# Chunk sums of the x1 squares on VectorE, norm rows and output tokens by other transposes, in a one-core streaming encoder layer

## The chip, the core and the metric

The kernel runs on one core of a Trainium2 chip. The metric is the device time in microseconds of one execution, taken as the median of several runs. The profile below is of one execution, recorded by the hardware profiler; its rows name instructions by the line of the kernel (L1307 is line 1307), by engine (PE is TensorE's matmul, PEld its weight load, DVE is VectorE, ACT is ScalarE, POOL is GpSimd, SP issues DMAs) and by the program's tile names.

## The reference, cut to what matters

One layer of an encoder works on 1024 prompt tokens and 32 sample tokens, 1056 in all, with 1024 features:

```
h = RMSNorm(x); z = h @ W_in                 # queries, keys, gates ...
A: windowed attention;  B: gated linear recurrence
m = sigmoid(gA) * (y_A @ W_brA) + sigmoid(gB) * (y_B @ W_brB)
x = x + RMSNorm(m @ W_out)                   # this x is "x1" in the kernel
[a | u] = RMSNorm(x) @ W_up;  a = causal depthwise conv3(a)
x = x + RMSNorm((gelu(a) * u) @ W_down)      # this x is "x2"
y = x + (p @ W_ple) * sigmoid(x @ W_ple_gate)
```

RMSNorm divides each token by the root of the mean of its squares over the 1024 features and scales each feature. All data are float32.

## The kernel before, in words

Inside the kernel the data lie transposed: features on the 128 partitions (1024 features are 8 chunks of 128) and tokens along the free dimension. Each product is split into high and low parts, so that each block of weights takes three matmuls (lines 202 to 204, 1735 to 1737, 2014 to 2016, 2105 to 2107). From the W_out product on, the 1056 tokens are four groups of 264 (`H`); groups 0 and 1 are a pair, and so are groups 2 and 3.

The instructions are not issued in the order of the text. A scheduler puts them in order on each engine, by their order in the text and by when its model thinks their inputs ready. `behind(engine)` (line 88) ties what it encloses, on that engine, behind the instruction of that engine that was traced last: it can't be issued earlier, but it waits for nothing else. `mm`, `tr` and `st` tiles are PSUM banks; there are two `tr` banks and three `st` pairs.

The parts that the change touches:

- **Norm rows** (`norm_rows`, line 298). A norm is a column: one value a token, tokens on partitions. The kernel needs it as rows, the same value on all 128 partitions. It takes the column, broadcast to 128 columns, as the weights of a matmul and the identity as the moving operand. It is called with three pieces for each group: at the start for the first RMSNorm (three groups of up to 3 x 128 tokens), by `pair_norm` (two groups of 3 x 88 tokens, so six calls; four pair norms in all) and by `x2_rows` (six calls, twice).
- **The x1 sums of the second pair.** `x1_half` (line 1329) adds the normed W_out product onto x; the result, x1 of groups 2 and 3, lies in `x1q[g]`, two halves of 4 chunks x 264 tokens, in a page of a large pool (`lq`) that an operand part of the up stage takes over later. `last_ops` (line 1698), called after each of the seven steps of the first half of up unit 0, squares it in place on ScalarE (line 1703, steps 2 and 4) and calls `x1_sums(2)` at step 5. `x1_sums` (line 1711) calls `sums88` (line 1302): for each of three pieces of 88 tokens, eight matmuls, one for each chunk, with the squares as weights and a single column of ones as the moving operand, accumulate the sum of squares into one PSUM column (line 1307). `x1_sums(3)` comes after the first step of the second half, then `pair_norm(1, ...)`: VectorE turns the sums into reciprocal roots (line 1318 and `rsqrt`, lines 213 to 219). The rows follow behind the fifth step. The first pair's squares are added over chunks on VectorE before the sums (`x1_squares`, line 1354).
- **Up unit 0** (`up_unit`, line 1717). 22 units make the up projection by seven products each (Strassen's scheme). Unit 0 is done in two halves, pair 0 then pair 1, each of seven steps of 12 matmuls, since pair 1's operands (`build_ops(1)`, lines 1379 and 1380) are still being made; `next(op1)` makes one part of them. After a step, `after` (line 1742) evacuates PSUM on VectorE (lines 1748, 1750, 1753, 1755, 1757, 1762, 1764). From the fifth step of the second half on, VectorE also prepares unit 1's weights.
- **The output stage** (line 2087). For each half h of the tokens and each chunk c of 128 features, 16 blocks in all, 48 matmuls with W_ple_gate, then tanh on ScalarE and two operations on VectorE give `y`, features on partitions, 2 x 264 tokens. One block later `y_done` (line 2054) turns it: six transposes of 88 tokens into two `tr` banks (line 2064), two ScalarE copies into `yr` tiles (line 2075), and, after each odd chunk, stores of two chunks' columns (lines 2077 to 2080) from SP's queue, which also loads the `ple` blocks (line 2043) and the x1 blocks (line 1949). The y tiles have the tag "t" with four buffers, shared with these x1 blocks. The very last block is turned piece by piece, so that its stores start early.

## Time and profile before

| | |
|---|---|
| median of three runs | 2006.07 us (2005.35 to 2007.28) |
| the profiled execution | 2008.97 us, of which its span 2006.5 us |
| mean granted TensorE clock over the span | 0.993 |
| up units (L1735) | 1192.2 to 1659 us |
| down product (L2014) | 1659.6 to 1893 us |
| output stage (L2105) | from 1893.5 us |
| mean DMA rate | 139 GB/s |

How to read it: the profile gives for each engine its busy time and the number of its instructions; "idle before, releaser" says how long the engine stood before an instruction and what it waited for. In a timeline row stand the start, the duration, engine, line, operation, written and read tiles, shapes and how many rows were merged. A matmul's duration includes its way through the array, which overlaps with the next one, so the cost of a matmul in the queue is the distance between starts, not the duration. A float32 product shows as two records of weight load and matmul where it isn't marked float32r, and a transpose as one.

### The profile page before, as it was taken

What the parts mean: (1) busy time and instruction counts of PE and PEld (TensorE: products, weight loads), DVE (VectorE), ACT (ScalarE), POOL (GpSimd) and SP (SyncE); (2) the same over time, 40 slices, a digit from 0 to 9 for tenths busy, and PEclk for the clock granted to TensorE, in tenths of its full rate; (3) what the DMA queues carried; (4) which work ended last, traced back from release to release, by engine and by line L of the source; (5) the groups of instructions that cost most, each with busy time, mean ns of one, the idle gap of its engine ahead of it and who ended that gap; (6) DMA issues with size and microseconds to landing.
All of it is one profiled execution on the core that took longest, in us unless ns stands there. A gap on an engine that the chain in (4) does not pass through costs nothing. (4 is left out here: it accounts for less than half of the span.)

```text
span 2006.5 us, 38869 instructions
## 1 busy us (share of the span) xinstructions
PE 1977.5 (99%) x14858; PEld 1946.1 (97%) x14858; DVE 1466.2 (73%) x3187; ACT 975.8 (49%) x2224; POOL 286.0 (14%) x386
## 2 busy tenths in 40 slices
PE   7999999999999999999999999999999998999998
PEld 6999999999999999999999999999999998999998
DVE  5788888688888888644455777787878886677852
ACT  5655556556666666542124653333333344534532
POOL 2010100000000000002100022545454431000000
PEclk9999999999999999999999998999999999999999
DMA  8322321321111111377656693564555669889543
GB/s 262 94 97 69 106 73 52 136 64 47 47 42 46 54 56 56 119 215 233 195 167 198 215 315 83 114 145 117 141 128 128 141 171 284 257 261 267 151 112 84
DMA packets 334498, 278.12 MB, mean 139 GB/s; under 512 B 15512, under 2 KB 317867, under 8 KB 333672
## 3 DMA queue, kind: packets, MB, share of 16 engines
q1 hardware_dynamic: 312114, 234.94, 39.3%
q0 software_dynamic: 22128, 40.65, 9.0%
q8 instruction: 116, 1.90, 0.4%
q14 instruction: 70, 0.57, 0.1%
q10 hardware_dynamic: 70, 0.06, 0.0%
HBM read 186.48 MB, written 89.11 MB: 137 GB/s over the span
## 5 line engine op out<-in xcount | busy, mean ns | idle before, releaser
L1735 PE MATMUL st<-op,wt 128*128 128x264 f32 x1232 | 352.1, 286 | 3.2 <-DVE Sp L1753 1.5
L1737 PE MATMUL st<-op,wt 128*128 128x264 f32 x1232 | 351.3, 285 | 0.0
L1736 PE MATMUL st<-op,wt 128*128 128x264 f32 x1232 | 349.6, 284 | 0.0
L1735 PEld LDWEIGHTS st<-op,wt 128*128 128x128 f32 x1232 | 233.1, 189 | 5.7 <-DVE Sp L1753 3.3
L1736 PEld LDWEIGHTS st<-op,wt 128*128 128x128 f32 x1232 | 233.2, 189 | 0.0
L1737 PEld LDWEIGHTS st<-op,wt 128*128 128x128 f32 x1232 | 232.7, 189 | 0.0
L2014 PE MATMUL st<-X,wd 128*128 128x264 f32 x616 | 175.2, 284 | 4.5 <-ACT wd L1817 4.5
L2016 PE MATMUL st<-X,wd 128*128 128x264 f32 x616 | 175.5, 285 | 0.6 <-DVE wd L1818 0.6
L2015 PE MATMUL st<-X,wd 128*128 128x264 f32 x616 | 174.7, 284 | 0.0
L202 PE MATMUL mm<-La,wh 128*128 128x384 f32 (+1 forms) x504 | 166.8, 332 | 0.3 <-ACT kt L342 0.3
L1517 ACT CAST wt<-wu 128x512 fp32r<-128x512 f32 x126 | 75.0, 619 | 181.8 <-POOL wu L1526 91.1
L203 PE MATMUL mm<-Lb,wh 128*128 128x384 f32 (+1 forms) x504 | 162.5, 322 | 0.0
L204 PE MATMUL mm<-La,wl 128*128 128x384 f32 (+1 forms) x504 | 162.5, 322 | 0.0
L202 PE MATMUL mm<-Ra,wh 128*128 128x264 f32 x512 | 145.4, 284 | 0.0
L204 PE MATMUL mm<-Ra,wl 128*128 128x264 f32 x512 | 145.1, 283 | 0.0
L203 PE MATMUL mm<-Rb,wh 128*128 128x264 f32 x512 | 145.0, 283 | 0.0
L1518 DVE TENSOR_TENSOR wt<-wu,wt 128x512 fp32r<-128x512 f32 x126 | 103.3, 821 | 48.2 <-ACT wt L1517 48.2
L2014 PEld LDWEIGHTS st<-X,wd 128*128 128x128 f32 x616 | 116.5, 189 | 4.7 <-ACT wd L1817 4.7
L2016 PEld LDWEIGHTS st<-X,wd 128*128 128x128 f32 x616 | 116.3, 189 | 1.1 <-DVE wd L1818 1.1
L2015 PEld LDWEIGHTS st<-X,wd 128*128 128x128 f32 x616 | 116.5, 189 | 0.0
L186 DVE TENSOR_TENSOR wl<-wr,wh 128x1024 fp32r<-128x1024 f32 x62 | 75.8, 1225 | 45.6 <-ACT wh L183 44.3
L455 ACT ACTIVATE sc<-sc,st 128x257 f32<-128x257 f32 (+1 forms) x144 | 69.7, 486 | 74.9 <-DVE st L450 73.7
(478 smaller groups left out, 6070.8 us busy)
## 6 DMA issues: line engine op xcount, KB each, us to landing
wq<-in_w_down_dram SPq DMA_DIRECT2D x96, 256.0 KB
wu<-in_w_up_dram SPq DMA_DIRECT2D x42, 512.0 KB
td<-Up SPq DMA_DIRECT2D x66, 264.0 KB
wu<-in_w_in_dram SPq DMA_DIRECT2D x32, 512.0 KB
X<-td SPq DMA_DIRECT2D x28, 528.0 KB
wr<-in_w_in_dram SPq DMA_DIRECT2D x26, 512.0 KB
td<-Up POOLq DMA_DIRECT2D x44, 264.0 KB, 5.9
wq<-in_w_down_dram SPq DMA_DIRECT2D x48, 192.0 KB
```

Source lines behind the costliest of these rows:

```text
L186: V.tensor_tensor(lo[:], raw[:], hi[:].bitcast(F32), op=ALU.subtract)
L202: E.matmul(ps, wh, a, start=first and n == 0, stop=False)
L203: E.matmul(ps, wh, b, start=False, stop=False)
L204: E.matmul(ps, wl, a, start=False, stop=last and n == len(ks) - 1)
L1517: S.copy(t[:, 0], src)
L1518: V.tensor_tensor(t[:, 1], src, t[:, 0].bitcast(F32), op=ALU.subtract)
L1735: E.matmul(o, wh, xh, start=first and k == 0, stop=False, skip_group_check=True)
L1736: E.matmul(o, wh, xl, start=False, stop=False, skip_group_check=True)
L1737: E.matmul(o, wl, xh, start=False, stop=k == 3, skip_group_check=True)
L2014: E.matmul(o, w[:, 0, k, :], x[:, 0, k, :], start=first, stop=False)
L2015: E.matmul(o, w[:, 0, k, :], x[:, 1, k, :], start=False, stop=False)
L2016: E.matmul(o, w[:, 1, k, :], x[:, 0, k, :], start=False, stop=last)
```

## The change

`norm_rows` makes its rows with `E.transpose` in place of a matmul; operands are the same. The squares of groups 2 and 3 come after steps 0 and 2 in place of 2 and 4. `x1_sums` first adds the eight chunks of squares into one on VectorE (4 + 4, 2 + 2, 1 + 1 chunks, behind VectorE's last traced instruction) and then sums one chunk, three matmuls a group in place of 24; `x1_sums(3)` comes one step later. `y_done` takes the 528 tokens of a block as one line for 14 of the 16 blocks (not the last two): four transposes of 128 tokens into one bank and one of 16 tokens into the other, one copy of 128 x 512 and one of 16 x 128, written over the y tile's first columns. The 16 tokens are stored for each block from the y tile; the rest after each odd chunk, as one store for the first 256 tokens and three or four for the others. The `yr` tiles have four rows of tokens in place of three and three buffers in place of four.

```
@@ norm_rows
-            E.matmul(t[:, c:c + m_], rs[:m_, i:i + 1].to_broadcast([m_, P]), ident[:m_, :m_],
-                     start=True, stop=True)
+            E.transpose(t[:, c:c + m_], rs[:m_, i:i + 1].to_broadcast([m_, P]), ident[:m_, :m_])
@@ last_ops
-        if n in (2, 4):
+        if n in (0, 2):
+            g = 2 + n // 2
             for i in range(2):
-                x = x1q[1 + n // 2][i]
+                x = x1q[g][i]
                 S.activation(x, x, AF.Square)
@@ x1_sums
+        x = x1q[g][0]
+        with behind(V):
+            V.tensor_tensor(x[:], x[:], x1q[g][1][:], op=ALU.add)
+            for n in (2, 1):
+                V.tensor_tensor(x[:, 0:n], x[:, 0:n], x[:, n:2 * n], op=ALU.add)
         with behind(E):
-            sums88(x1_t[0], g, [x1q[g][k // 4][:, k % 4, :] for k in range(KT)])
+            sums88(x1_t[0], g, [x[:, 0, :]])
@@ up_unit
-                if ps == (1,) and n == 0:
+                if ps == (1,) and n == 1:
                     x1_sums(3)
                     x1_t.append(pair_norm(1, 1.0 / D, x1_t[0]))
@@ new, before y_done
+    def y_spans(h):
+        spans = []
+        for p in range(2):
+            o = H * (2 * p + h)
+            for a, b in ((o, min(o + H, 1024)), (1024, o + H)):
+                if a < b:
+                    spans.append((a - o + H * p, b - o + H * p, a))
+        return spans
+
+    def y_store(h, i0, m, fc):
+        for a, b, t in y_spans(h):
+            a_, b_ = max(a, i0), min(b, i0 + m)
+            if a_ < b_:
+                t += a_ - a
+                dst = y_prompt[0, t:t + b_ - a_, fc] if t < 1024 else y_sample[0, t - 1024:t - 1024 + b_ - a_, fc]
+                yield a_ - i0, b_ - i0, dst
@@ y_done
+        if h == 0 or c < 6:
+            if c % 2 == 0:
+                yrs[0] = ep.tile([P, 4, 256], F32, tag="yr", name=nm("yr"), bufs=3)
+            yf = y[:].rearrange("p a b -> p (a b)")
+            t, x = tr_bank(), tr_bank()
+            for n in range(4):
+                E.transpose(t[:, n * P:(n + 1) * P], yf[:, n * P:(n + 1) * P], ident[:])
+            E.transpose(x[:16, 0:P], yf[:, 512:528], ident[:])
+            S.copy(yrs[0][:, :, col:col + P], t[:, :].rearrange("p (a b) -> p a b", b=P))
+            S.copy(yf[:16, 0:P], x[:16, 0:P])
+            for a, b, dst in y_store(h, 512, 16, slice(c * P, (c + 1) * P)):
+                dma(dst, yf[a:b, 0:P])
+            if c % 2:
+                o = H * h
+                dma(y_prompt[0, o:o + 256, fc].rearrange("(a p) c -> p a c", p=P), yrs[0][:, 0:2, :])
+                for n in (2, 3):
+                    for a, b, dst in y_store(h, P * n, P, fc):
+                        dma(dst, yrs[0][a:b, n, :])
+            return
         for p in range(2):
             if c % 2 == 0:
-                yrs[p] = ep.tile([P, 3, 256], F32, tag="yr", name=nm("yr"), bufs=4)
+                yrs[p] = ep.tile([P, 4, 256], F32, tag="yr", name=nm("yr"), bufs=3)
...
-            S.copy(yr[:88, :, col:col + P], t[:88, :3 * P].rearrange("p (a b) -> p a b", b=P))
+            S.copy(yr[:88, 0:3, col:col + P], t[:88, :3 * P].rearrange("p (a b) -> p a b", b=P))
```

## The prediction

> **What bounds the kernel now.** I read the page first (busy shares), then TensorE's waits, then its clock by stretches, then the timeline around each line that the change touches.

> ```profile
> span 2006.5 us, 38869 instructions
> ```
> ```profile
> PE 1977.5 (99%) x14858; PEld 1946.1 (97%) x14858; DVE 1466.2 (73%) x3187; ACT 975.8 (49%) x2224; POOL 286.0 (14%) x386
> ```
> ```profile
> PE st L2014 <- ACT wd L1817: 4.5, 1, 4.5
> PE st L1735 <- DVE Sp L1753: 1.5, 1, 1.5
> ```

> TensorE is busy 1977.5 of 2006.5 us, and past the first loads its longest waits are single ones of 4.5 and 1.5 us. So TensorE's queue sets the time, and a microsecond taken out of it is a microsecond of the kernel, unless another engine is late right there. All three edits take records out of that queue. The profiled execution took 2008.97 us, 2.5 more than its span and 2.9 more than the median of the three timed runs; the sum is a difference, so I make it on the profiled execution (2008.97) and state the forecast against the median (2006.07).

> Busy does not mean fast. The granted clock around the 48 column sums (columns: stretch in us; PE, PEld, DVE, ACT, POOL busy; PEclk; DMA):

> ```profile
> 1204.90:1208.30 3.40, 3.40 (x17) 3.40 (x17) 1.88 (x3) 2.02 (x2) 0.00 (x0) 0.50 0.17 43
> 1208.30:1211.70 3.40, 3.40 (x41) 3.40 (x41) 0.00 (x0) 0.51 (x2) 0.00 (x0) 1.00 0.02 5
> 1211.70:1218.50 6.80, 6.80 (x38) 6.80 (x38) 3.98 (x13) 1.45 (x2) 0.00 (x0) 0.50 0.00 0
> ...
> 1221.00:1242.60 21.60, 20.13 (x167) 19.80 (x165) 20.45 (x31) 10.81 (x19) 6.66 (x5) 1.00 0.24 73
> ```

> Two things to see: TensorE runs at half clock for 3.4 and then 6.8 us here, and directly behind it, from 1221 to 1242.6, VectorE is busy 20.45 of 21.6 us, so there VectorE has no room left.

> **Edit 1: the x1 sums.** Before, 24 products with a single moving column for each of two groups; each shows as two records, so x48 per group:

> ```profile
> 1200.90 0.28 PE L1737 MATMUL st<-op,wt 128*128 128x264 f32 x1
> 1201.02 3.85 PE L1307 MATMUL tr<-ones,x 128*88 128x1 f32 x48
> 1204.73 0.42 PE L1735 MATMUL st<-op,wt 128*128 128x264 f32 x1
> ```
> ```profile
> 1209.14 0.28 PE L1737 MATMUL st<-op,wt 128*128 128x264 f32 x1
> 1209.26 4.94 PE L1307 MATMUL tr<-ones,x 128*88 128x1 f32 x48
> 1214.06 0.57 PE L1735 MATMUL st<-op,wt 128*128 128x264 f32 x1
> ```

> They hold the queue for 1204.73 − 1201.02 = 3.71 and 1214.06 − 1209.26 = 4.80 us (the second partly at half clock). After the change each group has 3 products, 6 records. The same kind of sum after a chunk addition already stands in the trace, for the first norm of this pair of groups, 12 records for two groups:

> ```profile
> 1164.32 1.03 PE L1307 MATMUL tr<-ones,sqz 128*88 128x1 f32 x12
> 1165.21 0.37 PE L202 MATMUL mm<-pc,wh 128*128 128x264 f32 x1
> 1165.41 0.29 PE L203 MATMUL mm<-pc,wh 128*128 128x264 f32 x1
> ```

> 12 records take 0.89 us, so both groups together cost 0.89, and the saving in the queue is 8.51 − 0.89 = 7.6 us. The matmuls behind it run at the usual 0.12 us spacing once the switch is over (1165.41 on), so a burst this short doesn't cost the clock. The long ones do. Between the two bursts lie 24 matmuls (12 of the first half's last step, 12 of the second half's first): 1204.73 to 1209.26 is 4.53 us, where 24 × 0.12 = 2.88 are due: 1.65 lost. Behind the second burst the half clock lasts from 1214.06 to 1218.50: half of 4.44 is lost, 2.2. I take both as gone: 3.85. Together 11.45 us. [...]

> What it adds is VectorE's: per group an addition of 128x1056, one of 128x528, one of 128x264.

> ```profile
> L1384 DVE TENSOR_TENSOR z<-z,z x2: 1249/1252/1254, 1144.0 to 1183.8; 128x1056 f32<-128x1056 f32 x2
> ```
> ```profile
> L1748 DVE TENSOR_TENSOR Sp<-Sp,st x23: 430/692/701, 1195.5 to 1645.6; 128x528 f32<-128x528 f32 x21, 128x264 f32<-128x264 f32 x2
> ```

> 1.25 + 0.69 + 0.43 = 2.37 us, twice 4.75. They are queued behind the last VectorE instruction traced, so for the first group behind L1755:

> ```profile
> 1199.78 0.43 DVE L1755 TENSOR_TENSOR us<-Sp,st 128x264 f32<-128x264 f32 x1 [1.02 <-PE st L1737]
> 1201.22 0.43 DVE L1757 TENSOR_TENSOR us<-st,Sp 128x264 f32<-128x264 f32 x1 [1.01 <-PE st L1737]
> ...
> 1214.24 0.16 DVE L1318 TENSOR_SCALAR nv<-tr 88x6 f32<-88x6 f32 x1 [5.97 <-PE tr L1307]
> ...
> 1218.52 0.17 DVE L219 SCALAR_TENSOR_TENSOR nr<-rst,nr 128x6 f32<-128x6 f32 x1
> 1220.73 0.43 DVE L1748 TENSOR_TENSOR Sp<-Sp,st 128x264 f32<-128x264 f32 x1 [2.04 <-PE st L1737]
> ```

> They run from 1200.21 to about 1202.6, while TensorE finishes its step at 1201.02. The sums can't start before 1202.6, but the next step's 12 matmuls (12 × 0.12 = 1.44 us) need none of it and fill just this gap if they are issued first; I expect that, since their inputs are ready earlier. Behind the additions wait L1757 (it frees a PSUM bank first needed two steps into the second half) and the operand parts L1380, whose pages are free only after the sums; the second group's sums are moved one step later, which leaves 12 more matmuls as cover. That step is taken from the norm's way to its rows: L1318 to the last L219 took 1214.24 to 1218.69, 4.45 us with operand parts in between, and three steps (36 × 0.12 = 4.3 us) are left before the rows; the rows just fit, and what they are late is in VectorE's account next.

> Then VectorE's total. From 1201.0 to 1218.5 it was busy 0.43 + 1.88 + 0 + 3.98 = 6.3 us and then idle until 1220.73. With the additions that is 11.05; 0.8 us of it starts before 1201.0. TensorE now covers 1201.0 to 1220.73 in 19.7 − 11.45 = 8.3 us. VectorE arrives 11.05 − 0.8 − 8.3 = 2 us late at L1748, in front of the stretch where it has no slack. The 1.5 us wait for L1753 ends that stretch, so I let the 2 us come back there: +2.0. Ends: 0 (small instructions overlap, order changes) and 4.75 (nothing hidden). A gain below 0 is excluded, as VectorE only gets more work. The squares on ScalarE are moved, not added; before, they were done ahead of the first step and I cost them at nothing.

> Edit 1: −11.45 + 2.0 = −9.45 us.

> **Edit 2: norm rows by transposes.** Six products broadcast each pair's norm, two records each. The same shape as transposes stands in the trace too (p's columns, 88 x 128 weights, 88 moving columns), one record each:

> ```profile
> 1168.94 1.47 PE L303 MATMUL tr<-ident,nr 88*128 88x88 f32 x12
> 1170.20 0.37 PE L202 MATMUL mm<-pc,wh 128*128 128x264 f32 x1
> 1170.41 0.28 PE L203 MATMUL mm<-pc,wh 128*128 128x264 f32 x1
> ```
> ```profile
> 984.00 0.62 PE L1232 MATMUL tr<-ident,pr 88*128 88x88 f32 x6
> 984.41 0.37 PE L202 MATMUL mm<-Ya,wh 128*128 128x264 f32 x1
> 984.62 0.28 PE L203 MATMUL mm<-Yb,wh 128*128 128x264 f32 x1
> ```

> From the first record to the second ordinary matmul: 1.47 against 0.62 us, 0.85 saved for each set of six. There are six sets (four pair norms, two output norms): −5.1 us, all in TensorE's queue. That the weight is a broadcast column makes no difference to the product today; I assume none for the transpose. The three sets of three 128-wide calls at the kernel's start save one record of about 0.11 us a call, 1.0 us at most; TensorE waits for inputs in that stage, so I take a third, 0.35 (ends 0 and 1.0).

> **Edit 3: output transposes.** Six of 88 tokens become four of 128 and one of 16 in 14 of 16 blocks.

> ```profile
> 1920.72 0.82 PE L2064 MATMUL tr<-ident,y 128*88 128x128 f32 x6
> 1921.29 0.37 PE L2105 MATMUL st<-x,gw 128*128 128x264 f32 x1
> 1921.50 0.28 PE L2106 MATMUL st<-x,gw 128*128 128x264 f32 x1
> ```
> ```profile
> 427.39 0.49 PE L1006 MATMUL tr<-ident,ke 128*128 128x128 f32 x3
> 427.63 0.42 PE L838 MATMUL Z<-TH,wt 128*128 128x384 f32 x1
> ```

> Six cost 0.78 − 0.12 = 0.66 us, 0.11 each; three with 128 weight columns stand at the same spacing (0.82 us from first start to third end for six, 0.49 for three: (0.82 − 0.49) / 3 = 0.11). So price goes by the 128 moving columns, and a block saves one record: 14 × 0.11 = −1.5 us. The 16-token transpose costs a full one.

> The other engines are far off the bound in this stage:

> ```profile
> 1905.00:2006.00 101.00, 95.87 (x796) 94.71 (x794) 39.69 (x74) 27.85 (x62) 0.00 (x0) 0.99 0.36 98
> ```

> ScalarE, 27.85 of 101 us, gets one larger and one tiny copy for two middling ones. SP gets more stores: a small one per block and four or five for a pair of blocks instead of two or four. Each is queued ahead of later ple loads, and the longest store issue is 1.2 us:

> ```profile
> L2079 SPq DMA_DIRECT2D out_dram<-yr x3: 1192/1198/1207, 1968.3 to 1994.3; - x3
> ```

> Three or four more of these are under 5 us of issue in two blocks (about 13 us), and a ple buffer is loaded two blocks ahead: I cost it at nothing. The last two blocks, which end the kernel, keep the old form.

> **Sum:** −9.45 − 5.1 − 0.35 − 1.5 = −16.4 us. Profiled execution: 2008.97 to 1992.6; median: 2006.07 to 1989.7.

> **Rivals.**
> - *VectorE holds TensorE.* The sums are issued straight behind the step of 1200.90 and TensorE stands for 1.5 us in each group; with the sums this leaves some 1.5 of 3.4 us of real work, and the half clock comes again, 1.7 us a time. 2 × 3.2 = 6.4 lost instead of 2.0: 1994.1. For it: the old sums were issued exactly there. Against: they were ready then, the new ones aren't.
> - *The full additions land in the saturated stretch* (all of 4.75 us instead of 2.0): 1992.5. For: VectorE 20.45 of 21.6 us. Against: 2 + 5.97 us of idle time just before it.
> - *Broadcast transposes keep two records*, so edit 2 does nothing: 1989.7 + 5.45 = 1995.1. Against: no transpose row here has two.
> [...]
> - *Slower:* the y tile is now held until its 16-row store has landed, and in four blocks of the first half it shares four buffers with the x1 loads. If the landing comes later than the 6.5 us of a block, tanh waits for a buffer, the PSUM banks stay full and TensorE stands, up to a block each: 4 × 6.5 = 26 us, 2015.7. Against: 0.36 DMA share in this stage, and these loads have a block to spare.

> **How the numbers follow.** About 0.2% (4 us) is what a measurement of this kernel can tell from no change. Chances: forecast 0.58, VectorE holding TensorE 0.15, full additions 0.10, two records 0.04, transposes and clock 0.04, slower 0.04; 0.05 I leave to an instruction order changed elsewhere that eats the gain to within 4 us. Faster 0.91, same 0.05, slower 0.04. Range: the low end has nothing of the 2.0 come back, the whole 1.0 at the start, and the half clock behind the 4.5 us wait for L1817 shortened by a window (1.7): 1989.7 − 4.4 = 1985.3. The high end takes in the first three rivals: 1996.

> **What would show it.** Right: L1307 has 36 + 12 records instead of 132; PEclk 1.0 throughout 1200 to 1215; L303 has half its records, 0.62 us a set; L2064 and its successor 82; TensorE's wait for L1753 longer by up to 2 us; everything behind the second group's sums 9 to 15 us earlier. Wrong: TensorE waiting for VectorE at the sums, a 0.5 clock there, or waits in the last 100 us. The forecast fails if the order of work in the first up unit is laid out anew so that operand parts come late.

## The result and the profile after

| | before | after |
| --- | --- | --- |
| median of the timed runs, us | 2006.14 (2005.35 to 2007.28, 4 runs) | 1992.43 (1991.51 to 1992.73, 4 runs) |
| profiled execution, us | 2008.97 | 1991.51 |
| its span, us | 2006.5 | 1989.8 |

The ratio is 0.993, with a 95% interval of 0.9913 to 0.9948: 13.7 us faster. The forecast was 1989.7, 2.7 us lower, in a range of 1985.3 to 1996.0.

The page of the kernel after:

```profile
span 1989.8 us, 38642 instructions
PE 1956.4 (98%) x14715; PEld 1925.1 (97%) x14715; DVE 1468.6 (74%) x3193; ACT 972.5 (49%) x2224; POOL 282.6 (14%) x386
```

TensorE has 143 records less and is busy 21.1 us less, but the span fell by 16.7: some of what its queue lost came back as waits. TensorE's waits after (engine, line and releaser: us in total, times, the longest):

```profile
PE st L2019 <- ACT wd L1822: 5.5, 1, 5.5
PE st L1740 <- DVE x L1718: 1.7, 1, 1.7
PE st L1740 <- ACT ple L1487: 1.5, 2, 1.0
...
PE st L1740 <- DVE nr L219: 1.0, 1, 1.0
PE st L1740 <- DVE rst L217: 0.6, 1, 0.6
```

The 1.5 us wait for L1753 that ended VectorE's full stretch before is gone. New are 1.7 us, put down to an addition of the change (L1718), and 1.0 and 0.6 for the norm's small operations. The wait at the start of the down stage grew from 4.5 to 5.5. The sums themselves, in the timeline after:

```profile
1199.49 0.28 PE L1741 MATMUL st<-op,wt 128*128 128x264 f32 x1
1199.73 0.56 PE L1306 MATMUL tr<-ones,x 128*88 128x1 f32 x6
1200.15 0.37 PE L1740 MATMUL st<-op,wt 128*128 128x264 f32 x1
...
1203.87 0.60 PE L1306 MATMUL tr<-ones,x 128*88 128x1 f32 x6
1204.33 0.37 PE L1740 MATMUL st<-op,wt 128*128 128x264 f32 x1
```

0.42 and 0.46 us for 3.71 and 4.80. The stretches around them (us; PE, PEld, DVE, ACT, POOL busy; PEclk; DMA share; GB/s):

```profile
1185.00:1195.00 10.00, 8.51 (x68) 8.08 (x67) 5.78 (x8) 4.37 (x8) 0.00 (x0) 1.00 1.07 323
1195.00:1197.90 2.90, 1.21 (x11) 1.02 (x9) 2.72 (x5) 0.09 (x1) 0.00 (x0) 1.00 1.07 319
1197.90:1204.50 6.60, 6.60 (x58) 6.59 (x59) 4.61 (x7) 2.81 (x4) 0.00 (x0) 1.00 0.34 83
1204.50:1215.00 10.50, 8.89 (x72) 8.53 (x72) 10.03 (x30) 5.15 (x10) 0.00 (x0) 1.00 0.00 0
```

The clock is 1.00 throughout, as forecast. In the second row TensorE stands for 1.7 of 2.9 us, and two things end there: VectorE is nearly full (2.72 of 2.90), and the 16 DMA engines are full (1.07) up to just this point. Which of them held TensorE was the main question for the experiments.

The other two edits, a set of norm rows and one output block:

```profile
1898.08 0.62 PE L303 MATMUL tr<-ident,nr 88*128 88x88 f32 x6
1898.49 0.37 PE L2148 MATMUL st<-x,wh 128*128 128x264 f32 x1
...
1905.24 0.60 PE L2088 MATMUL tr<-ident,y 128*128 128x128 f32 x4
1905.67 0.27 PE L2089 MATMUL tr<-ident,y 128*16 128x128 f32 x1
1905.70 0.37 PE L2148 MATMUL st<-x,gw 128*128 128x264 f32 x1
```

From the first record to the matmul behind it, a set of rows takes 0.41 us (1170.20 − 1168.94 = 1.26 before), a block 0.46 (1921.29 − 1920.72 = 0.57 before): 0.85 and 0.11 saved, as priced.

**Where the time went, stage by stage.** I take the start of the first matmul of each stage from both timelines.

| stage | before | after | saved | forecast |
| --- | --- | --- | --- | --- |
| to TensorE's matmul at 100 us | 103.26 | 98.34 | 4.92 | 0.35 |
| to the first up matmul | 1088.94 | 1088.04 | 0.90 | 2.55 (3 sets) |
| to the first down matmul | 467.43 | 458.08 | 9.35 | 10.3 (9.45 and a set) |
| first 300 matmuls of the down stage | 44.08 | 45.19 | −1.11 | 0 |
| to the first gate matmul | 189.76 | 188.92 | 0.84 | 0.85 (a set) |
| to the end | 113.04 | 111.23 | 1.81 | 2.35 (a set and 1.5) |

Most of the first row is not the change's: in that profiled execution of the kernel before, the clock was at half from 41.0 to 47.8 us, which is 3.4 us lost, and in the one after it was not. Without that row the stages save 11.8 us, where 16.05 were forecast for them.

### The profile page after: what moved, and what is told of

It is laid out like the page before. It is cut to its first block, busy times and chain, and to the rows that moved or that the text cites. A ratio compares the mean times of both kernels' runs of the same rounds, so it can differ in the third digit from the quotient of the medians.

```text
span 1989.8 us, 38642 instructions
## 1 busy us (share of the span) xinstructions
PE 1956.4 (98%) x14715; PEld 1925.1 (97%) x14715; DVE 1468.6 (74%) x3193; ACT 972.5 (49%) x2224; POOL 282.6 (14%) x386
## 3 DMA queue, kind: packets, MB, share of 16 engines
q8 instruction: 115, 1.88, 0.4%
## 5 line engine op out<-in xcount | busy, mean ns | idle before, releaser
L202 PE MATMUL mm<-La,wh 128*128 128x384 f32 (+1 forms) x504 | 166.9, 332 | 0.3 <-ACT kt L341 0.3
L203 PE MATMUL mm<-Lb,wh 128*128 128x384 f32 (+1 forms) x504 | 162.6, 323 | 0.0
L202 PE MATMUL mm<-Ra,wh 128*128 128x264 f32 x512 | 145.4, 284 | 0.0
L203 PE MATMUL mm<-Rb,wh 128*128 128x264 f32 x512 | 145.0, 283 | 0.0
L186 DVE TENSOR_TENSOR wl<-wr,wh 128x1024 fp32r<-128x1024 f32 x62 | 75.8, 1224 | 46.0 <-ACT wh L183 44.5
```

The lines of the kernel that those rows point to most:

```text
L186: V.tensor_tensor(lo[:], raw[:], hi[:].bitcast(F32), op=ALU.subtract)
L202: E.matmul(ps, wh, a, start=first and n == 0, stop=False)
L203: E.matmul(ps, wh, b, start=False, stop=False)
```

## The experiments

All twelve are compared with the kernel before on the same chip. There were three such groups (e0 to e3; e8, e4, e5 and e7; e9 to e12), with 2006.92, 2006.21 and 2008.08 us for the kernel before, so medians are compared within a group and ratios across groups. The up stage is the time from the first up matmul to the first down matmul in the run's profile; it leaves out what the clock does in the first 60 us. "Wait" is TensorE's before the last step (n = 6) of the first half of up unit 0, and half clock is counted from 1185 to 1222 us.

| kernel | median us (runs) | ratio, 95% interval | up stage | wait | half clock |
| --- | --- | --- | --- | --- | --- |
| before, its own runs | 2006.14 (4) | | 467.4 | 0 | 10.2 |
| after, first runs | 1992.43 (4) | 0.993, 0.9913 to 0.9948 | 458.1 | 1.70 | 0 |
| e0_before | 2007.23 (12) | 1.0003, 0.9989 to 1.0017 | 467.1 | 0 | 10.2 |
| e1_sums | 2001.56 (8) | 0.9972, 0.9957 to 0.9987 | 464.1 | 2.64 | 6.8 |
| e2_rows | 2002.63 (12) | 0.998, 0.9969 to 0.9992 | 469.6 | 0 | 13.7 |
| e3_out | 2003.32 (10) | 0.998, 0.9971 to 0.9989 | 465.7 | 0 | 6.8 |
| e8_after | 1994.53 (6) | 0.9939, 0.9923 to 0.9956 | 462.0 | 2.53 | 6.8 |
| e4_raw_late | 1990.49 (6) | 0.9916, 0.99 to 0.9931 | 456.4 | 0 | 0 |
| e5_no_adds | 1993.98 (6) | 0.9935, 0.9919 to 0.995 | 461.1 | 2.48 | 3.4 |
| e7_four_chunks | 2001.65 (12) | 0.9973, 0.9962 to 0.9984 | 464.4 | 2.49 | 3.4 |
| e9_raw_late_again | 1991.54 (6) | 0.9915, 0.9898 to 0.9931 | 456.3 | 0 | 0 |
| e10_four_chunks_raw_late | 1995.18 (6) | 0.9932, 0.9917 to 0.9947 | 461.9 | 0 | 3.4 |
| e11_no_adds_raw_late | 1991.75 (5) | 0.9914, 0.9899 to 0.993 | 457.5 | 0 | 0 |
| e12_before_raw_late | 2007.12 (12) | 0.9994, 0.9983 to 1.0004 | 468.9 | 0 | 13.7 |

The theory: the last step before the first group's sums waits for its weight tile. The tile is loaded behind the raw weights of the next unit on full DMA engines (share 1.07 in the profile after), and before, the long sums stood exactly in that gap. The rival: VectorE's new additions hold TensorE, as the page's releaser says and as the prediction priced.

**The kernel before again, and each edit alone.**

> The kernel before, unchanged, profiled a second time. Theory (early clock): the half clock from 41 to 48 us in the first profile was that execution's own; here it is absent or shorter, and the span is 2003 to 2005 us, 2 to 3.4 below the first profile. Rival (early gain belongs to the change): the half clock is there again, the span is 2006 to 2007 us.

No edit. The median is that of before, but the profiled execution took 2016.29 us. Its clock was at half from 38.6 to 52.2 us; my expectation that this early stretch was a chance of the first profile and would be gone was wrong: it came again, 13.7 us long in place of 6.8.

> Only the x1 sums of the change. Prediction's sum: 9.45 us faster than before. Theory (cover lost): 7.5 to 9 us faster; the 48-record bursts and both half clocks are gone, but TensorE stands 1.5 to 3 us before the last step of the first half because that step's weights are still on their way. Rival (VectorE holds TensorE): 5 us faster or less, with waits for the additions and a half clock behind them.

```
-        if n in (2, 4):
+        if n in (0, 2):
...
+            V.tensor_tensor(x[:], x[:], x1q[g][1][:], op=ALU.add)
+            for n in (2, 1):
+                V.tensor_tensor(x[:, 0:n], x[:, 0:n], x[:, n:2 * n], op=ALU.add)
...
-            sums88(x1_t[0], g, [x1q[g][k // 4][:, k % 4, :] for k in range(KT)])
+            sums88(x1_t[0], g, [x[:, 0, :]])
...
-                if ps == (1,) and n == 0:
+                if ps == (1,) and n == 1:
```

5.6 us by the ratio (2.6 to 8.6), where 9.45 was forecast. The wait before step n = 6 is 2.64 us here, and 6.8 us of half clock follow it. So edit 1 alone has the new wait, and it costs more than in the first profile after.

> Only the norm rows by transposes. Prediction's sum: 5.1 + 0.35 = 5.45 us faster. Theory (early clock): 4 to 5.5 us faster, since each of the six sets takes 0.62 us in place of 1.47 and some of it is lost where TensorE waits for ScalarE's copies. Rival (early gain belongs to the change): 8 to 10 us faster, with the first 100 us shorter by over 4.

```
-            E.matmul(t[:, c:c + m_], rs[:m_, i:i + 1].to_broadcast([m_, P]), ident[:m_, :m_],
-                     start=True, stop=True)
+            E.transpose(t[:, c:c + m_], rs[:m_, i:i + 1].to_broadcast([m_, P]), ident[:m_, :m_])
```

4.0 us (1.6 to 6.2), against 5.45 forecast: one record a transpose, 36 for 72, and the size agrees within the interval.

> Only the output transposes of 128 tokens. Prediction's sum: 1.5 us faster. Theory: 1.2 to 1.6 us faster, 0.11 a block for 14 blocks. Rival (stores and held y tiles): no gain or slower, with TensorE waiting in the last 100 us.

The edit is `y_done` alone, as in the change's diff. 4.0 us (2.2 to 5.8), against 1.5. Its profile doesn't show that much in its own stage. From the first gate matmul to the last it takes 105.81 us against 105.67 before, and holds a wait that the first profile of before doesn't have:

```profile
PE st L2144 <- DVE x L226: 1.5, 1, 1.5
```

Without that wait, 1.3 us are saved, which is the forecast's size. The same wait stands in the second profile of before (1.6 us, at the same line of the gate matmuls), so it isn't the edit's. TensorE's instructions ahead of the gate stage are the same in both kernels; where the other 2 to 3 us of the medians come from stays open. Some of it may be the clock: the long sums, which this edit leaves as they are, brought 10.2, 10.2, 13.7, 6.8 and 13.7 us of half clock in the five profiles that have them (before, e0, e2, e3, e12), and e3 happens to have the least.

The three gains, 5.6, 4.0 and 4.0, add up to 13.6, the whole change to 13.7 (11.7 beside e8). With intervals of 2 to 3 us to either side of each, this shows no hold of one edit on another, but could not show one of a few us.

**Is the wait the weight tile's or VectorE's?**

> The changed kernel once more, beside the three below. If what its first runs showed is of the kernel and not of one execution: median 1991.5 to 1994, and in its profile again one wait of 1.4 to 2.0 us in front of the last step of the first half of up unit 0 (step n=6, near 1197 us), no half clock between 1185 and 1215, and a wait of 5 to 6 us at the start of the down stage with 6.8 us of half clock behind it. Half clock in the first 60 us may come or stay away in any execution (0 to 13.7 us of it in the profiles so far) and is no part of the change.

No edit. 2 us slower than the first runs. Its profile is of an execution of 1999.91 us, 5.4 above the median, so it is read by stages; it shows why the time of this kernel isn't settled by one execution:

```profile
1196.96 1.17 DVE L1718 TENSOR_TENSOR x<-x 128x528 f32<-128x528 f32 x2
...
1199.04 0.36 PE L1740 MATMUL st<-op,wt 128*128 128x264 f32 x1 [2.53 <-DMA wt<-fw_d]
```

The wait is 2.53 us now. VectorE's additions end at 1198.13, 0.9 us before TensorE goes on, and the releaser is now the weight tile's load. In the first profile after, the tile landed at 1197.70 and the addition ended at 1197.76, 0.06 us apart: the page took the later one. What follows the longer wait:

```profile
1196.60:1199.04 2.44, 0.00 (x0) 0.03 (x1) 1.49 (x4) 0.00 (x0) 0.00 (x0) 1.00 1.06 308
1200.00:1206.80 6.80, 6.80 (x35) 6.80 (x34) 4.50 (x7) 2.43 (x3) 0.00 (x0) 0.50 0.16 39
```

Half clock for 6.8 us, 3.4 lost, before the sums have even been issued (1201.70). I had expected none: wrong. The first wait of the down stage is 4.6 us, where I had expected 5 to 6.

> The changed kernel with the raw weight loads of up unit 1 (two of 512 KB) issued behind the last weight tile of unit 0 and not behind its fourth. Theory A (the 1.7 us wait in front of step n=6 is a late weight tile: its load was issued at 1190.45 and landed at 1197.70, queued behind these raw loads; the old sums had hidden it): the wait falls below 0.5 us, the kernel is 1 to 2 us faster than the changed one, about 1991, as long as unit 1's first parts are still in time; if these come late the wait moves to the start of unit 1 and the time stays. Theory B (the wait is VectorE, whose evacuation at L1718 is the releaser that the page names, late because of the chunk additions): the wait stays at 1.7 us and the time within 0.5 us.

```
-                if i == 3:
+                if i == 6:
                     unit_raw(1)
```

The wait is gone and so is the half clock; 4.0 us faster than the changed kernel beside it. SP's queue, first of the kernel after, then of this one's second run (e9):

```profile
1189.01 1.35 SPq L1505 DMA_DIRECT2D wu<-in_w_up_dram  x2
1190.45 2.02 SPq L1550 DMA_DIRECT2D wt<-fw_d  x1
```
```profile
1192.16 0.37 SPq L1550 DMA_DIRECT2D wt<-fw_d  x1
1192.62 6.49 SPq L1505 DMA_DIRECT2D wu<-in_w_up_dram  x4
```

The up stage starts 3.15 us later in e9 (first up matmul at 1189.53, in the kernel after at 1186.38), so both are counted from there. The tile is issued at 2.63 us here, ahead of the raw weights, and at 4.07 there, behind two of their loads; it lands at 7.91 against 11.31. Step n = 6 is due at 9.6, and in e9 it starts straight behind step 5, at full clock:

```profile
1199.01 0.29 PE L1742 MATMUL st<-op,wt 128*128 128x264 f32 x1
1199.13 0.28 PE L1740 MATMUL st<-op,wt 128*128 128x264 f32 x1
```
```profile
1195.00:1205.00 10.00, 10.00 (x86) 9.88 (x85) 7.54 (x13) 2.99 (x4) 0.00 (x0) 1.00 0.96 246
```

VectorE's additions are the same in both.

> The changed kernel without the six additions on VectorE: the sums are taken over the squares of one chunk of eight, which leaves out the other seven in the second pair's x1 norm. Everything else stays. Theory A (late weight tile): the 1.7 us wait in front of step n=6 stays, 1.3 to 2.0 us; what goes are the waits that VectorE causes further on (0.6 at the norm's factor, 1.0 at an evacuation), so 0.5 to 1.6 us faster than the changed kernel. Theory B (VectorE's additions hold TensorE in front of n=6): 1.70 + 0.60 + 1.00 go together, 2.5 to 3.5 us faster. In the prediction the lateness of VectorE was priced at 2.0 us, which is between.

```
-        with behind(V):
-            V.tensor_tensor(x[:], x[:], x1q[g][1][:], op=ALU.add)
-            for n in (2, 1):
-                V.tensor_tensor(x[:, 0:n], x[:, 0:n], x[:, n:2 * n], op=ALU.add)
```

```profile
1196.08 0.56 PE L1306 MATMUL tr<-ones,x 128*88 128x1 f32 x6
1199.12 0.36 PE L1736 MATMUL st<-op,wt 128*128 128x264 f32 x1 [2.48 <-DVE op L1379]
```

There is no addition left, the sums are even done ahead of the step, and the wait still stands: 2.48 us. The page names yet another VectorE instruction for it, which ends at 1199.04; the tile lands at 1198.98, again 0.06 us ahead. Theory B falls: these additions are not the cause. 0.55 us between the medians is inside the noise.

**What do the additions cost, and how short must the sums be?** These stand on the order of loads without the wait.

> The changed kernel with unit 1's raw weights issued behind unit 0's last weight tile, once more, beside the three below that are built on this order. If its first runs showed the kernel: median 1989 to 1992, no wait over 0.5 us in front of step n=6 of unit 0, no half clock between 1185 and 1215.

As expected: 1991.54, no wait, no half clock. With e4, twelve runs of this order give ratios of 0.9916 and 0.9915; the changed kernel gave 0.993 and 0.9939. The intervals overlap; the up stage, 456.4 and 456.3 against 458.1 and 462.0, does not. The difference is the wait and what follows from it: 458.1 less its 1.70 us is 456.4, and 462.0 less 2.53 us and less 3.4 us lost at half clock is 456.1. It is the fastest version here that sums all eight chunks.

> The same with none of the six additions on VectorE; the sums are taken over one chunk of eight, which leaves out seven eighths of the squares. Theory A (the additions lie beside other work and cost nothing; VectorE's short waits behind them come with the order of its queue, not with its load): within 1 us of the kernel with raw weights late, and 1.5 to 2.5 us of short waits for VectorE are still there between 1185 and 1300, under whatever names. Theory B (VectorE is late by the additions, 2.0 us in the prediction): 1.6 to 2.5 us faster, and the waits of 0.6 and 1.0 us are gone with nothing in their place.

The four lines that e5 takes out, and e4's edit. 1991.75 against 1991.54 for the kernel beside it: six additions of 4.75 us together cost nothing that the runs show. The medians alone, known to 3 us to either side, could not tell 2 us; the up stage can, and it is no shorter without the additions (457.5 against 456.4 and 456.3). TensorE's waits for VectorE are still there, in other places:

```profile
PE st L1736 <- DVE Sp L1749: 1.5, 2, 1.0
...
PE st L1736 <- DVE Up L1756: 0.7, 1, 0.7
```

2.2 us here, 1.0 + 0.6 with the additions: so the additions' load does not make them; that the order in VectorE's queue does is what theory A says, and nothing here tests it. Theory B falls here too.

> The changed kernel with only the first of the three additions of a group on VectorE (128x1056), and the sums over the four chunks that are left: 12 products, 24 records a group instead of 6, and 1.1 us less of VectorE a group. 24 records take 24 x 0.077 = 1.9 us against 0.5: +1.4 us a group, 2.8 in all. Theory C (it needs about a whole window of 3.4 us of single-column products before the clock halves): clock 1.0 throughout 1185 to 1215, 1.5 to 2.8 us slower than the changed kernel. Rival D (any burst near 2 us tips a window): a stretch of 3.4 or 6.8 us at half clock behind one group or both, another 1.7 to 3.4 us, 4 to 6 us slower in all.

```
-            for n in (2, 1):
-                V.tensor_tensor(x[:, 0:n], x[:, 0:n], x[:, n:2 * n], op=ALU.add)
...
-            sums88(x1_t[0], g, [x[:, 0, :]])
+            sums88(x1_t[0], g, [x[:, k, :] for k in range(4)])
```

7.1 us slower than the changed kernel beside it, more than either theory gave; in the profiles the up stage is only 2.4 us longer (464.4 against 462.0), and where the rest comes from stays open. As the 2.49 us wait stood in front of the sums, this couldn't tell whether the 3.4 us of half clock came from the wait or from the burst; e10 was made for that.

> The same with only the first of the three additions of a group on VectorE and sums over four chunks: 24 records a group instead of 6, with no wait for a weight tile near them. Theory C (a burst of 1.9 us alone does not halve the clock; the half clock of the four-chunk kernel before came from its 2.5 us wait for the weight tile): clock 1.0 throughout 1185 to 1220, 1.5 to 4 us slower than the kernel beside it (2.8 of records, and whatever VectorE's changed order does). Rival D (the burst alone does it): a half-clock stretch behind one group or both, 3 to 7 us slower.

e7 and e4 together. 3.6 us slower than e9. The first burst and the stretches behind it:

```profile
1199.12 2.01 PE L1306 MATMUL tr<-ones,x 128*88 128x1 f32 x24
1200.99 0.37 PE L1738 MATMUL st<-op,wt 128*128 128x264 f32 x1
```
```profile
1201.70:1205.10 3.40, 3.40 (x18) 3.40 (x17) 2.82 (x4) 1.62 (x2) 0.00 (x0) 0.51 0.45 108
1205.10:1208.50 3.40, 3.40 (x38) 3.40 (x36) 1.12 (x1) 0.76 (x2) 0.00 (x0) 0.99 0.00 0
```

1.87 us of products with a single column, no wait near them, and the granted clock behind them is 0.51 for 3.4 us: theory C falls, rival D holds for this group. Behind the second group's burst (1206.97 to 1208.80, 1.83 us) the matmuls start 0.12 us apart, at full clock: of two bursts near 1.9 us, one was followed by half clock and one was not. Counted back and on from the change of the clock at 1201.74 in steps of 3.41 us, the length of this half clock, the first burst lies whole in one step (1198.33 to 1201.74), and the second is shared by two, 1.60 and 0.23 us (last section).

> The kernel before, with unit 1's raw weights issued behind unit 0's last weight tile. Theory A (before, the 3.7 us of sums stood exactly where the weight tile was late, so the late tile cost nothing there): within 1 us of the kernel before, 2005 to 2007, and still two half-clock stretches between 1195 and 1222, 10 us together, from the sums. Rival (the order of the loads is worth 2 to 4 us by itself, whatever the sums do): 2002 to 2004.

e4's edit in the kernel before. Within 1 us, and the two half-clock stretches of the sums are there, 13.7 us together:

```profile
1200.80:1207.60 6.80, 6.80 (x36) 6.80 (x36) 1.88 (x3) 2.15 (x2) 0.00 (x0) 0.50 0.24 60
1207.60:1211.00 3.40, 3.40 (x46) 3.40 (x45) 0.00 (x0) 0.38 (x1) 0.00 (x0) 1.00 0.02 5
1211.00:1217.80 6.80, 6.80 (x34) 6.80 (x34) 4.14 (x14) 1.45 (x2) 0.00 (x0) 0.50 0.00 0
```

By the ratio the order of the loads is worth 1.2 us here, from −0.8 to 3.4; the profiles have nothing that it could mend, as no wait stands in front of step n = 6 in either. So the late tile cost nothing while the long sums covered it, and the gain of e4 is the cover that the change took away. In the first profile of before, the tile was issued behind two raw loads on full DMA engines (share 1.08):

```profile
1193.86 1.20 SPq L1506 DMA_DIRECT2D wu<-in_w_up_dram  x2
1195.15 2.92 SPq L1551 DMA_DIRECT2D wt<-fw_d  x1
```
```profile
1190.00:1200.90 10.90, 10.16 (x83) 9.94 (x83) 5.07 (x7) 4.41 (x9) 0.00 (x0) 1.00 1.08 327
```

It landed at 1204.23, and its step began at 1204.73, straight behind the sums.

## Why the prediction was right, and what in it was not

- **The sums' records (−7.6): right.** 8.51 to 0.88 us, where 0.89 was taken from the sums of the other pair.
- **The clock (−3.85): right in kind, not safe.** With no wait in front of the sums there is no half clock in three of three profiles with the short sums (e4, e9, e11). In the first profile after, none followed a wait of 1.7 us; in e8 it followed one of 2.5 us, and 3.4 us of the gain were gone again. What there was to gain is no fixed size either: 6.8 to 13.7 us of half clock came with the long sums, so 3.4 to 6.8 us.
- **The step that failed** is the sentence that the next step's 12 matmuls "need none of it" and fill the gap, "since their inputs are ready earlier". They need none of the additions, and were put in the gap; but their weight tile was not there. The evidence was in the trace of before: a load on full DMA engines (share 1.08), issued behind 512 KB loads, for a step that began just behind a 3.7 us burst. I looked at VectorE for what would be late next, and not at the loads. It cost 1.7 to 2.6 us, and half clock on top where it was long.
- **VectorE's lateness (+2.0, ends 0 and 4.75): the low end was right.** The waits of 1.0 and 0.6 us stand against a wait of 1.5 us that went, and with the additions taken out the time is the same (e11). The 2.0 was the right size for the wrong cause: the tile's wait took its place in the sum, and the forecast of the stage, 10.3 us, came near the 9.35 of the first profile after for that reason. That was luck: in e8 the same stage saved 5.4.
- **Norm rows (−5.1 − 0.35): price right, cover missed.** A set saves 0.85 us where TensorE is the bound. The three sets ahead of the up stage saved 0.9 us together in the first profile after, and not 2.55; there TensorE also waits for loads and for ScalarE (0.2 to 1.4 us in these profiles). That stretch, from the matmul at 100 us to the first up matmul, takes 1087.0 to 1090.6 us in the nine profiles with the new rows and 1088.7 to 1089.4 in the five without. In five of the nine (e4, e5, e7, e8, e10) TensorE waits there 1.9 to 2.2 us for a weight tile that VectorE makes (L186), in none of the five without; why, and why not in all nine, stays open. Alone the edit gave 4.0 us.
- **Output transposes (−1.5): right by the rows**, 0.11 a block; the medians of e3 alone show 2.2 to 5.8, which its own stage doesn't explain.
- **What wasn't in the sum:** the start of the down stage gave 1.1 us back in the first profile after, where its first wait grew from 4.5 to 5.5 us. That is of the execution, not of the change: in e8 the wait is 4.6 us and the first 300 matmuls take 43.65 us, 0.4 less than before. 6.8 us of half clock stand behind the wait in all three (1689.6 to 1696.4 before, 1676.2 to 1683.0 after). The range's low end took 1.7 us off that half clock; none of them shows this term, the 6.8 us stayed.
- **The rivals.** VectorE holding TensorE at the sums did not happen, though the 1.7 us wait looked like it. The doubled records did not happen: 36 records for six sets. Nor did the slower case: the last stage has no wait of TensorE over 0.5 us in the first profile after, and the 1.8 us that it has in e8 stand at the line (L226) that the second profile of before waits for too, 1.6 us. The chance of 0.04 given to transposes and the clock did not come about either: in the first profile after the clock is 1.00 from 24.2 to 1676.1 us and from 1683.1 to 1986.7, and all six sets of rows (1119.3 to 1898.5) and the 14 blocks of 128-token transposes (1891.6 to 1975.8) lie there.

In total 12 us of the 16.4 are in the first profile after (13.7 by its medians, 11.7 by those beside e8). With the late tile mended (e4, e9) the medians are 15.7 and 16.5 us below before: about the sum's 16.4. That it is met so closely is partly luck, as the 2.0 of VectorE was not there and the rows ahead of the up stage gave less than their 2.55.

## What to carry to other kernels

Before taking a burst out of a busy queue, look for what arrives while it runs: here a late load that cost nothing under 3.7 us of sums became a wait of 1.7 to 2.6 us without them (DMA share 1.07 in the first profile after), and no wait when it was issued ahead of the raw loads (e4, e9; share 0.96 in e9). When the releaser that a page names ended within 0.1 us of another candidate, take each of them away in a run of its own. Measure a stage from its first instruction to the next stage's first, if the whole time moves between executions for other reasons.
